# Opening of a hybrid attention and state-space layer: first weight unit laid out by k step, x and norm weights fetched on other queues, other splits and warm-up products

## The chip, the cores and the metric

The kernel runs on one core of one Trainium2 chip. The metric is the device time of one execution in microseconds (us). TensorE is called PE, VectorE DVE, ScalarE ACT, GpSimd POOL and SyncE SP, as in the profile. SP, ACT and POOL each have a queue on which they issue DMA transfers.

## The reference, cut to what matters

One layer on `x` of 256 rows by 2048 columns, batch 1, all in float32:

```python
hn = rms_norm(x, norm_w)
proj = hn @ w_in          # 2048 x 20544: q, k, v, z_a, z_s, xbc, dt, g_a, g_s
...                       # three dilated attentions, a convolution and a chunked state scan
merged = sigmoid(g_a) * (o_a @ w_attn_branch) + sigmoid(g_s) * (y @ w_ssm_branch)
return rms_norm(x + merged @ w_out, final_norm_w)
```

The change touches only the first product with `w_in`: 512 of its columns (one block of 128 for each of B, C, x and z of the state-space branch), against all 2048 rows of the contraction.

## The kernel before

**Weights and splits.** All weights lie in one array `wall` of units of 128 x 1024 floats (512 KB). Every unit is fetched by one transfer on SP's queue (`load`, L267) into one of five buffers `w`. As the products work in `fp32r`, a rounded form, each unit is split: ACT writes the rounded part `h` (L278) and DVE the remainder `l` (L279). The activations are split likewise into a high and a low half that lie side by side, 256 columns each. For each block of 128 x 128 weights PE then does one product of `h` with both halves (512 columns) and one of `l` with the high half alone (256 columns).

**The first gemm.** `gemm_first` does the 512 columns in eight units. A unit holds two k steps, a k step being 128 rows of the contraction: its first 512 columns are the first step's, the other 512 the second's. A k step is eight products, `h` at L385 and `l` at L386, for four accumulators. The first four units are split in halves, a k step each (`N_FINE`). For each k step the x block must have been fetched (`xr`), scaled with that step's column of the norm weights `pk` and split: ACT writes the high half (L286), DVE the low half (L290). These are the tiles `yTa` and `yTb`. The row norm itself is applied later.

**The order at the start.** Transfers are issued in the order of the code: on SP's queue the norm weights `pk`, then in turn a half of unit 0, an x block, the other half, and so on; the first x block alone goes on ACT's queue (`N_ACT_X`). Before the data arrives PE does `N_WARM` products with a tile of zeros, `ssq`, that DVE sets. A scheduler sets each engine's order within the limits of the data; `in_order` keeps an instruction's place in the program.

Of the kernel before, what the change touches and what calls it, by code (L numbers as in the profile page):

```python
# [9 lines left out]
F32 = mybir.dt.float32  # L10
F32R = mybir.dt.float32r
AF = mybir.ActivationFunctionType
ALU = mybir.AluOpType
PSUM = bass.MemoryType.PSUM

P = 128
S = 256
# [6 lines left out]
KT = D // P  # L24
UNIT = 1024
UK = 8
UB = 2
# [2 lines left out]
M_AHEAD = 200  # L30
T_LAGS = 1, 1
W_BUFS, H_BUFS = 5, 4
N_WARM = 4
X_CUTS = ((0, 1), (1, 2), (2, 4), (4, 6), (6, 8), (8, 10))
N_FINE = 4
N_ACT_X = 1
DT_LAG, CB_LAG, TURN_LAG, Y_LAG, S_LAG, M_LAG = 2, 8, 3, 11, 2, 2
# [88 lines left out]
FIRST = {}  # L126
# [6 lines left out]
def lay_weights(mats):  # L133
    out = np.empty((N_UNITS, P, UNIT), np.float32)
    for tag, form, src, off, n_kt, w in PLAN:
        if form == "m":
            m = np.concatenate([mats[src][:, o : o + P] for o in off], axis=1)
        else:
            m = mats[src][:, off : off + w]
        uk = UNIT // w  # L140
        n = n_kt // uk
        if form == "p":


            m = m.reshape(n // 2, 2, P, 2, 512)
            for q in range(n // 2):
                f = FIRST[tag] + 2 * q
                if q in S_QUADS[tag]:
                    out[f] = np.concatenate([m[q, 0, :, 0], m[q, 1, :, 0]], axis=1)
                    out[f + 1] = np.concatenate([m[q, 0, :, 1], m[q, 1, :, 1]], axis=1)  # L150
                else:
                    out[f : f + 2] = m[q].reshape(2, P, UNIT)
            continue
        out[FIRST[tag] : FIRST[tag] + n] = m.reshape(n, uk, P, w).transpose(0, 2, 1, 3).reshape(n, P, UNIT)
    return out


# [41 lines left out]
def hybrid_block(ctx: ExitStack, tc: tile.TileContext, wall, xt, x, pk_d, cst_d, fw_d, out):  # L199
    nc = tc.nc  # L200
    ve, ac, gp, pe = nc.vector, nc.scalar, nc.gpsimd, nc.tensor
    in_order = tc.keep_in_program_order
# [9 lines left out]
    pk = lead.tile([P, N_PK], F32, name="pk", tag="pk")  # L212
# [13 lines left out]
    def bank(tag, bufs, name):  # L226
        return ps.tile([P, 512], F32, name=name, tag=tag, bufs=bufs)

    loaded = {}
# [7 lines left out]
    def ring(name):  # L237
        return stream.tile([P, UNIT], F32, name=name, tag="w", bufs=W_BUFS)
# [24 lines left out]
    def load(n, cuts=(0, UNIT)):  # L263
        if n not in loaded:
            loaded[n] = stream.tile([P, UNIT], F32, name=f"w{n}", tag="w", bufs=W_BUFS)
        for a, b in zip(cuts, cuts[1:]):
            nc.sync.dma_start(loaded[n][:, a:b], wall[n, :, a:b])  # L267

    def unit(n, shape):
        if n not in loaded:  # L270
            load(n)
        w = loaded.pop(n)
        h = stream.tile([P, UNIT], F32R, name=f"h{n}", tag="h", bufs=H_BUFS)
        l = stream.tile([P, UNIT], F32R, name=f"l{n}", tag="l", bufs=H_BUFS)
        cuts = (0, UNIT // 2, UNIT) if n < N_FINE else (0, UNIT)
        with tc.high_priority(L_AHEAD) if n >= KT // UB else nullcontext():
            for a, b in zip(cuts, cuts[1:]):
                ac.activation(h[:, a:b], w[:, a:b], AF.Copy)  # L278
                ve.tensor_tensor(l[:, a:b], w[:, a:b], h[:, a:b].bitcast(F32), ALU.subtract)  # L279
        for f in on_unit.pop(n, ()):  # L280
            f(h[:, 0:1].bitcast(F32))
        k, m = shape
        return h.rearrange("p (k m) -> p k m", k=k), l.rearrange("p (k m) -> p k m", k=k)

    def split(src, hi, lo, scale=1.0):
        ac.activation(hi, src, AF.Copy, scale=scale)  # L286
        if isinstance(scale, float):
            ve.tensor_tensor(lo, src, hi.bitcast(F32), ALU.subtract)
        else:
            ve.scalar_tensor_tensor(lo, src, scale, hi.bitcast(F32), ALU.mult, ALU.subtract)  # L290
# [4 lines left out]
    def kt_of(t, kt):  # L295
        return t[kt // 8][:, kt % 8, :] if isinstance(t, list) else t[:, kt, :]
# [21 lines left out]
    def tick(final=False):  # L318
        now[0] += 1
        run_due(float("inf") if final else now[0])  # L320

    def gemm_a(tag, xs_of, acc=None):
        run = 2 if tag in IN_TWOS else 1
        held = in_order if tag not in FREE else lambda ins: None
        tick()
        name = f"{tag[0]}{tag[1]}"
        acc = bank(acc, 2, f"ps_{name}") if acc else bank("g", 4, f"ps_{name}")
        for u in range(KT // UK):
            h, l = unit(FIRST[tag] + u, (UK, P))
            for k0 in range(0, UK, run):  # L330
                for kk in range(k0, k0 + run):
                    kt = u * UK + kk
                    high = pe.matmul(acc, h[:, kk, :], xs_of(kt), start=(kt == 0), stop=False)  # L333
                    if kt == 0:
                        held(high)
                        run_due(now[0] + 0.5)
                for kk in range(k0, k0 + run):
                    kt = u * UK + kk
                    low = pe.matmul(acc[:, S:], l[:, kk, :], xs_of(kt)[:, :S], start=False, stop=(kt == KT - 1))  # L339
        held(low)  # L340
        return acc
# [25 lines left out]
    def project(tag, acc=None):  # L367
        return gemm_a(tag, lambda kt: XT[:, kt, :], acc)

    def gemm_first(tag, prepare, load_on):  # L370
        name = f"{tag[0]}{tag[1]}"
        accs = [bank("g", 4, f"ps_{name}_{j}") for j in range(4)]
        for u in range(KT // UB):
            if u % 2 == 0:
                tick()
            for kk in range(UB):
                prepare(u * UB + kk)
            h, l = unit(FIRST[tag] + u, (UB, 512))
            load_on(u)
            for kk in range(UB):  # L380
                kt = u * UB + kk
                m = kt_of(yT, kt)
                for j, acc in enumerate(accs):
                    js = slice(j * P, (j + 1) * P)
                    pe.matmul(acc, h[:, kk, js], m, start=(kt == 0), stop=False)  # L385
                    pe.matmul(acc[:, S:], l[:, kk, js], m[:, :S], start=False, stop=(kt == KT - 1))  # L386
        return accs

    def evac(acc, out_ap, name, scale=1.0):
# [228 lines left out]
    xr = big.tile([P, KT, S], F32, name="xr", tag="yo1a")  # L618
# [3 lines left out]
    def half_kts(name, tag):  # L622
        return big.tile([P, KT // 2, 2 * S], F32R, name=name, tag=tag)

    yT = [half_kts(f"yT{n}", f"yo0{n}") for n in "ab"]
    ssq = cpool.tile([P, 2, S], F32, name="ssq", tag="ssq")
    ve.memset(ssq, 0.0)
    warm = bank("m2", 2, "warm")
    for _ in range(N_WARM):
        pe.matmul(warm[:, :S], ssq[:, 0, :P], ssq[:, 0], start=True, stop=True)  # L630
    th_s = big.tile([P, 2, D], F32, name="th_s", tag="sgs")
    nc.sync.dma_start(pk[:, :KT], pk_d[:, :KT])
    for n, (a, b) in enumerate(X_CUTS):
        (nc.scalar if n < N_ACT_X else nc.sync).dma_start(xr[:, a:b, :], xt[:, a:b, :])
        if n < 2:
            load(0, (n * UNIT // 2, (n + 1) * UNIT // 2))
        elif n < 5:
            load(n - 1)
    ac.activation(a_neg, half[:SH, 0:1], AF.Exp)

    def split_x(kt):
        split(xr[:, kt], kt_of(yT, kt)[:, :S], kt_of(yT, kt)[:, S:], scale=pk[:, kt : kt + 1])

    def fetch(dst, src, behind, queue=nc.sync):
        gp.tensor_copy(dst[:, 0:1], behind)
        queue.dma_start(dst, src)
# [7 lines left out]
    def load_on(u):  # L654
        if u:
            load(u + 4)
        if u < 3:
            nc.sync.dma_start(xr[:, 2 * u + 10 : 2 * u + 12, :], xt[:, 2 * u + 10 : 2 * u + 12, :])
        if u == 3:
            nc.sync.dma_start(pk[:, KT:], pk_d[:, KT:])  # L660
# [31 lines left out]
    with tc.tile_pool(name="ssm", bufs=2) as sp:  # L692
# [175 lines left out]


        accs = gemm_first(("first", 0), split_x, load_on)  # L870
        raws = [collect(acc, f"first{j}") for j, acc in enumerate(accs[:3])]
        first = {n: new_pair(0, n) for n in ("xs", "zs")}
# [50 lines left out]
        for g in range(GROUPS):  # L923
# [9 lines left out]
            for t in range(max(4 * g, 1), 4 * g + 4):  # L933
                u, i = divmod(t, 2)
                acc = project(("xs", t))
# [19 lines left out]
                acc = project(("zs", t))  # L955
# [88 lines left out]
    with tc.tile_pool(name="att", bufs=2) as ap:  # L1044
# [55 lines left out]
        for h in range(NH):  # L1100
            q, k = (ap.tile([P, S], F32, name=f"{n}T{h}", tag=f"{n}T", bufs=2) for n in "qk")
# [3 lines left out]
            p = ap.tile([P, 384], F32, name=f"p{h}", tag="p", bufs=2)  # L1105
# [21 lines left out]
    with tc.tile_pool(name="fin", bufs=2) as fp:  # L1127
# [36 lines left out]
        for n in range(4):  # L1164
            i, cs = n // 2, slice(n % 2 * UNIT, (n % 2 + 1) * UNIT)
            behind_unit(
                FIRST[X_BEHIND[n][0]] + X_BEHIND[n][1],
                lambda behind, i=i, cs=cs: fetch(fin[:, i, cs], x[i * P : (i + 1) * P, cs], behind, nc.scalar),
# [3 lines left out]
        for n, (tag, u) in enumerate(FW_BEHIND):  # L1172
            cs = slice(n * UNIT, (n + 1) * UNIT)
# [12 lines left out]
        for c0 in (0, 2):  # L1186
# [17 lines left out]
            for i in range(2):  # L1204
                f = fs[:, i, :9]
                for c, acc in zip((c0, c0 + 1), es[2 * i : 2 * i + 2]):
                    cs = slice(c * 512, (c + 1) * 512)
# [28 lines left out]
        for i in range(2):  # L1236
            r = fs[:, i, 7:8]
            for c in (3, 0, 2, 1) if i else (3, 0, 1, 2):
                cs = slice(c * 512, (c + 1) * 512)
# [43 lines left out]
```

## Time and profile before

| | us |
|---|---|
| median of three runs | 1380.45 |
| lowest, highest | 1379.41, 1380.56 |
| the profiled execution's own time | 1379.87 |
| its span, first to last instruction | 1378.0 |

The profile is of one execution, the 1379.87 us one; 1.87 us of it lie outside its span. All times of rows count from the span's start. PE is busy for 1366.8 us of the span (99%), DVE for 1177.0, ACT for 840.0, POOL for 161.7. The granted clock of TensorE is told in the profile as a share of 2.4 GHz.

### The profile page before, as it was taken

How to read it: one execution, taken by the hardware profiler on the slowest of the kernel's cores; microseconds unless marked ns; L12 is line 12 of the kernel's file. 1: busy time of each engine (PE TensorE's matmuls, PEld its weight loads, DVE VectorE, ACT ScalarE, POOL GpSimd, SP SyncE). 2: the span in 40 equal slices, each digit the busy share in tenths (PEclk: the TensorE clock that was granted, in tenths of full speed). 3: DMA queues.
4: the chain of work that ended last, by engine and by line, in shares of the span. 5: the costliest groups of instructions: out<-in, count | busy, mean ns of one | idle time of the engine just before them, and what ended most of it. 6: DMA issues, size and time to landing. Idle time of an engine off the chain costs nothing.

```text
span 1378.0 us, 20734 instructions
## 1 busy us (share of the span) xinstructions
PE 1366.8 (99%) x7260; PEld 1164.8 (85%) x7260; DVE 1177.0 (85%) x1763; ACT 840.0 (61%) x1310; POOL 161.7 (12%) x238
## 2 busy tenths in 40 slices
PE   9999999999999999999999999999999999999997
PEld 7888888888888888888888888888888888888886
DVE  6898899898899888788989888777877789988897
ACT  7655777675667676666565554454444557655564
POOL 2301211101020100010001001211211000400112
PEclk9999999999999999999999999999999999999999
DMA  9767878778787867578677568888889757875773
GB/s 342 237 190 237 298 267 286 262 244 288 248 277 237 298 203 220 174 242 277 228 261 270 211 215 316 306 275 280 306 298 302 230 163 267 291 244 173 246 273 122
DMA packets 106520, 348.15 MB, mean 253 GB/s; under 512 B 11888, under 2 KB 14256, under 8 KB 106416
## 3 DMA queue, kind: packets, MB, share of 16 engines
q1 hardware_dynamic: 104400, 340.67, 74.0%
q10 hardware_dynamic: 1440, 4.06, 0.8%
q0 software_dynamic: 576, 2.10, 0.4%
q8 instruction: 57, 0.93, 0.3%
q14 instruction: 47, 0.39, 0.1%
HBM read 316.97 MB, written 29.82 MB: 252 GB/s over the span
## 4 chain that ended last, share of the span: by engine, by line
PE 98%; DMA 0%; DVE 0%; ACT 0%; issue 0%; SPq 0%; POOL 0%; POOLq 0%; DVEq 0%
PE ps_xs L333 8%; PE ps_zs L333 8%; PE ps_k L333 4%; PE ps_za L333 4%; PE ps_q L333 4%; PE ps_zs L339 4%; PE ps_xs L339 4%; PE ps_ssm L485 3%; PE ps_ssm L486 3%; PE ps_ssm L484 3%; PE ps_q L339 2%; PE ps_za L339 2%; PE ps_k L339 2%; PE ps_gs L421 2%; PE ps_gs L422 2%; PE ps_gs L420 2%
## 5 line engine op out<-in xcount | busy, mean ns | idle before, releaser
L278 ACT ACTIVATE h<-w 128x1024 fp32r<-128x1024 f32 (+1 forms) x394 | 410.0, 1048 | 306.0 <-issue 73.7
L279 DVE TENSOR_TENSOR l<-w,h 128x1024 fp32r<-128x1024 f32 (+1 forms) x394 | 474.0, 1209 | 111.1 <-ACT h L278 106.9
L333 PE MATMUL ps_zs<-XT,h 128*128 128x512 f32 x496 | 172.0, 393 | 0.0
L333 PE MATMUL ps_xs<-XT,h 128*128 128x512 f32 x496 | 171.6, 393 | 0.0
L339 PE MATMUL ps_zs<-XT,l 128*128 128x256 f32 x496 | 134.6, 279 | 0.0
L339 PE MATMUL ps_xs<-XT,l 128*128 128x256 f32 x496 | 133.7, 277 | 0.0
L333 PEld LDWEIGHTS ps_xs<-XT,h 128*128 128x128 f32 x496 | 91.3, 188 | 19.4
L333 PEld LDWEIGHTS ps_zs<-XT,h 128*128 128x128 f32 x496 | 91.3, 188 | 18.9
L339 PEld LDWEIGHTS ps_zs<-XT,l 128*128 128x128 f32 x496 | 93.3, 188 | 2.1
L339 PEld LDWEIGHTS ps_xs<-XT,l 128*128 128x128 f32 x496 | 93.2, 188 | 2.1
L333 PE MATMUL ps_q<-XT,h 128*128 128x512 f32 x256 | 91.1, 404 | 0.0
L333 PE MATMUL ps_k<-XT,h 128*128 128x512 f32 x256 | 88.6, 395 | 0.0
L333 PE MATMUL ps_za<-XT,h 128*128 128x512 f32 x256 | 88.4, 394 | 0.0
L551 ACT ACTIVATE ha<-wa 128x1024 fp32r<-128x1024 f32 x45 | 47.5, 1056 | 45.9 <-PE ps_ssm L486 10.0
L339 PE MATMUL ps_q<-XT,l 128*128 128x256 f32 x256 | 68.4, 278 | 0.0
L339 PE MATMUL ps_k<-XT,l 128*128 128x256 f32 x256 | 68.4, 277 | 0.0
L339 PE MATMUL ps_za<-XT,l 128*128 128x256 f32 x256 | 68.4, 277 | 0.0
L552 DVE TENSOR_TENSOR la<-wa,ha 128x1024 fp32r<-128x1024 f32 x45 | 54.8, 1218 | 8.4 <-ACT ha L551 8.3
L552 DVE TENSOR_TENSOR ltu<-wa,htu 128x1024 fp32r<-128x1024 f32 x40 | 48.7, 1219 | 10.8 <-ACT htu L551 10.8
L793 ACT ACTIVATE gt<-acb,acT 128x128 f32<-128x128 f32 x128 | 44.1, 390 | 22.2 <-DMA acb<-acum_d 21.9
L333 PEld LDWEIGHTS ps_k<-XT,h 128*128 128x128 f32 x256 | 47.0, 188 | 9.9
L333 PEld LDWEIGHTS ps_q<-XT,h 128*128 128x128 f32 x256 | 47.1, 188 | 9.7
(691 smaller groups left out, 3347.8 us busy)
## 6 DMA issues: line engine op xcount, KB each, us to landing
w<-in_wall SPq DMA_DIRECT2D x390, 512.0 KB, 4.8
wa<-in_wall SPq DMA_DIRECT2D x45, 512.0 KB, 4.7
th_a<-in_wall SPq DMA_DIRECT2D x21, 512.0 KB, 4.7
sums_at<-in_wall SPq DMA_DIRECT2D x18, 512.0 KB, 5.0
acb<-acum_d SPq DMA_DIRECT2D x32, 256.0 KB, 3.8
t_ssm<-sums_at SPq DMA_DIRECT2D x13, 512.0 KB, 4.3
wt<-t_ssm SPq DMA_DIRECT2D x13, 512.0 KB, 4.7
th_a<-in_wall SPq DMA_DIRECT2D x21, 256.0 KB, 5.4
```

The source lines that it names most:

```text
L278: ac.activation(h[:, a:b], w[:, a:b], AF.Copy)
L279: ve.tensor_tensor(l[:, a:b], w[:, a:b], h[:, a:b].bitcast(F32), ALU.subtract)
L333: high = pe.matmul(acc, h[:, kk, :], xs_of(kt), start=(kt == 0), stop=False)
L339: low = pe.matmul(acc[:, S:], l[:, kk, :], xs_of(kt)[:, :S], start=False, stop=(kt == KT - 1))
L420: pe.matmul(accs[i], xh, h[:, kk], start=(kt == 0), stop=False)
L421: pe.matmul(accs[i], xh, l[:, kk], start=False, stop=False)
L484: pe.matmul(acc, xh, h, start=start, stop=False)
L485: pe.matmul(acc, xh, l, start=False, stop=False)
L486: pe.matmul(acc, xl, h, start=False, stop=stop)
L551: ac.activation(h, src, AF.Copy)
L552: ve.tensor_tensor(l, src, h.bitcast(F32), ALU.subtract)
L793: ac.activation(g4[:, n, b], acb[:, j, b // 2 * P : b // 2 * P + P], AF.Relu, scale=-1.0, bias=sc[:, h : h + 1],)
```

## The change

- **Unit 0** lies in `wall` by k step: the 128 x 512 floats of its first k step are one run of 256 KB, then those of the second. Before, the two steps' rows of 2 KB alternated. Each half is still one transfer of 256 KB.
- **x** blocks 0 and 1 come in one transfer of 256 KB on ACT's queue, instead of one of 128 KB there and one on SP's.
- **Norm weights** `pk` (8 KB) are issued by POOL's queue instead of SP's.
- **Splits of x blocks 0 and 1** are both done by DVE: a multiplication with a scalar for the high half, in the place of ACT's, then the low half as before. DVE's order in unit 0 is written out: high, low, `l` for the first step, then for the second.
- **Products** of the first two k steps are written in a fixed order: four with `h`, then four with `l`.
- **Warm-up:** six products of 128 x 128 instead of four of 128 x 256, on a part of the zeros that is set first; the other zeros are set behind them.

```diff
-N_WARM = 4
-X_CUTS = ((0, 1), (1, 2), (2, 4), (4, 6), (6, 8), (8, 10))
+N_WARM = 6
+X_CUTS = ((0, 2), (2, 4), (4, 6), (6, 8), (8, 10))
...
+        if form == "m":
+            out[FIRST[tag]] = m[: uk * P].reshape(P, UNIT)
...
-            for a, b in zip(cuts, cuts[1:]):
+            for i, (a, b) in enumerate(zip(cuts, cuts[1:])):
+                if ahead:
+                    ahead(i)
                 ac.activation(h[:, a:b], w[:, a:b], AF.Copy)
-                ve.tensor_tensor(l[:, a:b], w[:, a:b], h[:, a:b].bitcast(F32), ALU.subtract)
+                low = ve.tensor_tensor(l[:, a:b], w[:, a:b], h[:, a:b].bitcast(F32), ALU.subtract)
+                if ahead:
+                    in_order(low)
...
-    ve.memset(ssq, 0.0)
+    ve.memset(ssq[:, 0, :P], 0.0)
     warm = bank("m2", 2, "warm")
     for _ in range(N_WARM):
-        pe.matmul(warm[:, :S], ssq[:, 0, :P], ssq[:, 0], start=True, stop=True)
+        pe.matmul(warm[:, :P], ssq[:, 0, :P], ssq[:, 0, :P], start=True, stop=True)
+    ve.memset(ssq[:, 0, P:], 0.0)
+    ve.memset(ssq[:, 1], 0.0)
     th_s = big.tile([P, 2, D], F32, name="th_s", tag="sgs")
-    nc.sync.dma_start(pk[:, :KT], pk_d[:, :KT])
+    gp.dma_start(pk[:, :KT], pk_d[:, :KT])
+    loaded[0] = ring("w0")
+    steps = wall[0].rearrange("(k p) (q m) -> k (p q) m", k=2, q=2)
+    for k in range(2):
+        nc.sync.dma_start(loaded[0][:, k * 512 : k * 512 + 512], steps[k])
     for n, (a, b) in enumerate(X_CUTS):
         (nc.scalar if n < N_ACT_X else nc.sync).dma_start(xr[:, a:b, :], xt[:, a:b, :])
-        if n < 2:
-            load(0, (n * UNIT // 2, (n + 1) * UNIT // 2))
-        elif n < 5:
-            load(n - 1)
+        if 0 < n < 4:
+            load(n)
     ac.activation(a_neg, half[:SH, 0:1], AF.Exp)
 
     def split_x(kt):
+        if kt < 2:
+            hi, lo = kt_of(yT, kt)[:, :S], kt_of(yT, kt)[:, S:]
+            in_order(ve.tensor_scalar(hi, xr[:, kt], pk[:, kt : kt + 1], None, ALU.mult))
+            ve.scalar_tensor_tensor(lo, xr[:, kt], pk[:, kt : kt + 1], hi.bitcast(F32), ALU.mult, ALU.subtract)
+            return
         split(xr[:, kt], kt_of(yT, kt)[:, :S], kt_of(yT, kt)[:, S:], scale=pk[:, kt : kt + 1])
```

SP's queue at the start, before: `w_93` is unit 0, `w_98` unit 1, `w_101` unit 2, `w_104` unit 3.

```order
L632 DMA pk<-in_pk 128x16
L267 DMA w_93<-in_wall 128x512
L634 DMA xr<-in_xt 128x256
L267 DMA w_93<-in_wall 128x512
L634 DMA xr<-in_xt 128x512
L267 DMA w_98<-in_wall 128x1024
L634 DMA xr<-in_xt 128x512
L267 DMA w_101<-in_wall 128x1024
```

The same place after the change: `w_96` is unit 0, `w_101` unit 1, `w_104` unit 2.

```order
L652 DMA w_96<-in_wall 128x512 x2
L654 DMA xr<-in_xt 128x512
L269 DMA w_101<-in_wall 128x1024
L654 DMA xr<-in_xt 128x512
L269 DMA w_104<-in_wall 128x1024
L654 DMA xr<-in_xt 128x512
```

Two transfers of the first five are gone from this queue, so unit 1 stands fourth in it instead of sixth; the others keep their order.

DVE at the start, before: zeros, then low halves of x and remainders `l` in turn.

```order
L627 MEMSET ssq 128x512
L290 SCALAR_TENSOR_TENSOR yTa<-xr,pk,yTa 128x256
L279 TENSOR_TENSOR l_131<-w_93,h_130 128x512
L290 SCALAR_TENSOR_TENSOR yTa<-xr,pk,yTa 128x256
L279 TENSOR_TENSOR l_131<-w_93,h_130 128x512
L290 SCALAR_TENSOR_TENSOR yTa<-xr,pk,yTa 128x256 x2
L279 TENSOR_TENSOR l_161<-w_98,h_160 128x512 x2
```

DVE at the start, after: `l_130` is of unit 0, `l_164` of unit 1.

```order
L641 MEMSET ssq 128x128
L645 MEMSET ssq 128x128
L646 MEMSET ssq 128x256
L662 TENSOR_SCALAR yTa<-xr,pk 128x256
L663 SCALAR_TENSOR_TENSOR yTa<-xr,pk,yTa 128x256
L283 TENSOR_TENSOR l_130<-w_96,h_129 128x512
L662 TENSOR_SCALAR yTa<-xr,pk 128x256
L663 SCALAR_TENSOR_TENSOR yTa<-xr,pk,yTa 128x256
L283 TENSOR_TENSOR l_130<-w_96,h_129 128x512
L296 SCALAR_TENSOR_TENSOR yTa<-xr,pk,yTa 128x256 x2
```

The multiplications of x blocks 0 and 1 have come from ACT to DVE, where each now stands ahead of its low half. On every engine the order of the rest of the program is the same as before but for a few neighbours that change places: the last transfers of x and two of the norm's products among them.

## Rows read from the trace of the kernel before

**Rows 1.** The page: the chain of work that ended last, by engine.

```profile
PE 98%; DMA 0%; DVE 0%; ACT 0%; issue 0%; SPq 0%; POOL 0%; POOLq 0%; DVEq 0%
```

**Rows 2.** PE alone in two stretches: length, busy (instructions), granted clock, DMA share, GB/s.

```profile
0.00:9.53 9.53, 6.73 (x25) 1.00 0.77 231
9.53:34.00 24.47, 24.47 (x133) 1.00 1.02 385
```

**Rows 3.** The chain that ended last, first 40 us: start, us, what.

```profile
3.07 5.75 DMA w<-in_wall
8.85 0.64 ACT h L278
9.53 1.20 PE ps_first L385 x4
...
12.60 0.93 PE ps_first L385 x4
13.53 0.47 PE ps_first L386 x4
```

**Rows 4.** Timeline: start, us, engine, line, operation, [idle time before it and its releaser].

```profile
0.72 0.10 POOL L224 MEMSET half<- 128x2 f32 x1 [0.29 <-POOLq L1273]
...
0.73 0.39 SPq L632 DMA_DIRECT2D pk<-in_pk  x1
...
1.18 0.41 SPq L267 DMA_DIRECT2D w<-in_wall  x1
...
1.44 3.68 PE L630 MATMUL warm<-ssq 128*128 128x256 f32 x8 [1.44 <-DVE ssq L627]
...
3.79 0.48 DVE L290 SCALAR_TENSOR_TENSOR yTa<-xr,pk,yTa 128x256 fp32r<-128x256 f32 x1 [2.40 <-ACT yTa L286]
3.87 0.63 ACT L278 ACTIVATE h<-w 128x512 fp32r<-128x512 f32 x1
...
4.54 0.69 DVE L279 TENSOR_TENSOR l<-w,h 128x512 fp32r<-128x512 f32 x1 [0.27 <-ACT h L278]
...
4.66 1.39 PE L385 MATMUL ps_first<-yTa,h 128*128 128x512 f32 x4
...
6.81 1.19 PE L385 MATMUL ps_first<-yTa,h 128*128 128x512 f32 x4 [0.29 <-ACT h L278]
```

**Rows 5.** DMA issues near 0.73, 1.18, 3.07 and 4.02 us: KB, us to landing.

```profile
pk<-in_pk SPq DMA_DIRECT2D x1, 8.0 KB, 2.3
...
w<-in_wall SPq DMA_DIRECT2D x1, 256.0 KB, 2.7
...
w<-in_wall SPq DMA_DIRECT2D x1, 512.0 KB, 5.8
...
w<-in_wall SPq DMA_DIRECT2D x1, 512.0 KB, 7.2
```

**Rows 6.** Four stretches, all engines: busy (instructions), then granted clock, DMA share, GB/s.

```profile
1.80:2.25 0.45, 0.45 (x2) 0.36 (x2) 0.00 (x0) 0.45 (x1) 0.00 (x0) 1.00 0.51 103
2.50:3.50 1.00, 1.00 (x4) 0.82 (x3) 0.00 (x0) 0.43 (x2) 0.00 (x0) 1.00 0.99 358
3.50:5.00 1.50, 1.50 (x6) 1.20 (x5) 0.95 (x2) 1.01 (x3) 0.43 (x1) 1.00 0.94 202
5.00:9.00 4.00, 3.17 (x17) 2.41 (x15) 2.29 (x5) 2.08 (x5) 0.27 (x1) 1.00 0.96 298
```

**Rows 7.** DMA issues of the whole span by line: 512 KB from POOL's queue and from SP's.

```profile
sx_x<-sxd_x SPq DMA_DIRECT2D x5, 512.0 KB, 5.1
...
sx_o<-sxd_o POOLq DMA_DIRECT2D x4, 512.0 KB, 7.9
```

**Rows 8.** Groups by line and shape on DVE: count, busy us, mean ns of one.

```profile
L1070 DVE TENSOR_SCALAR p<-p,st 128x256 f32<-128x256 f32 x16 | 5.6, 347 | 0.0
```

**Rows 9.** Groups of weight loads in the first 40 us.

```profile
L385 PEld LDWEIGHTS ps_first<-yTb,h 128*128 128x128 f32 x32 | 5.7, 188 | 1.0
...
L630 PEld LDWEIGHTS warm<-ssq 128*128 128x128 f32 x8 | 2.5, 331 | 2.0 <-DVE ssq L627 1.4
```

More of the change, by code (lines that the diff above doesn't have):

```diff
@@ L267, in load, with unit @@
             nc.sync.dma_start(loaded[n][:, a:b], wall[n, :, a:b])
-    def unit(n, shape):
+    def unit(n, shape, ahead=None):
         if n not in loaded:
@@ L375, in gemm_first @@
                 tick()
-            for kk in range(UB):
-                prepare(u * UB + kk)
-            h, l = unit(FIRST[tag] + u, (UB, 512))
+            if u:
+                for kk in range(UB):
+                    prepare(u * UB + kk)
+            h, l = unit(FIRST[tag] + u, (UB, 512), prepare if u == 0 else None)
             load_on(u)
@@ L382, in gemm_first @@
                 m = kt_of(yT, kt)
[L383 to L386, printed above, removed]
+                per = 4 if kt < 2 else 1
+                for j0 in range(0, 4, per):
+                    js = [(accs[j], slice(j * P, (j + 1) * P)) for j in range(j0, j0 + per)]
+                    for acc, cs in js:
+                        high = pe.matmul(acc, h[:, kk, cs], m, start=(kt == 0), stop=False)
+                        if kt < 2:
+                            in_order(high)
+                    for acc, cs in js:
+                        low = pe.matmul(acc[:, S:], l[:, kk, cs], m[:, :S], start=False, stop=(kt == KT - 1))
+                        if kt < 2:
+                            in_order(low)
         return accs
@@ L626, in hybrid_block @@
     ssq = cpool.tile([P, 2, S], F32, name="ssq", tag="ssq")
-    ve.memset(ssq, 0.0)
+    ve.memset(ssq[:, 0, :P], 0.0)
     warm = bank("m2", 2, "warm")
     for _ in range(N_WARM):
-        pe.matmul(warm[:, :S], ssq[:, 0, :P], ssq[:, 0], start=True, stop=True)
+        pe.matmul(warm[:, :P], ssq[:, 0, :P], ssq[:, 0, :P], start=True, stop=True)
+    ve.memset(ssq[:, 0, P:], 0.0)
+    ve.memset(ssq[:, 1], 0.0)
     th_s = big.tile([P, 2, D], F32, name="th_s", tag="sgs")
-    nc.sync.dma_start(pk[:, :KT], pk_d[:, :KT])
+    gp.dma_start(pk[:, :KT], pk_d[:, :KT])
[3 more added lines that the diff above has]
+        nc.sync.dma_start(loaded[0][:, k * 512 : k * 512 + 512], steps[k])
     for n, (a, b) in enumerate(X_CUTS):
         (nc.scalar if n < N_ACT_X else nc.sync).dma_start(xr[:, a:b, :], xt[:, a:b, :])
-        if n < 2:
-            load(0, (n * UNIT // 2, (n + 1) * UNIT // 2))
-        elif n < 5:
-            load(n - 1)
+        if 0 < n < 4:
+            load(n)
     ac.activation(a_neg, half[:SH, 0:1], AF.Exp)
     def split_x(kt):
+        if kt < 2:
+            hi, lo = kt_of(yT, kt)[:, :S], kt_of(yT, kt)[:, S:]
+            in_order(ve.tensor_scalar(hi, xr[:, kt], pk[:, kt : kt + 1], None, ALU.mult))
+            ve.scalar_tensor_tensor(lo, xr[:, kt], pk[:, kt : kt + 1], hi.bitcast(F32), ALU.mult, ALU.subtract)
+            return
         split(xr[:, kt], kt_of(yT, kt)[:, :S], kt_of(yT, kt)[:, S:], scale=pk[:, kt : kt + 1])
```

## Prediction

> **What bounds the kernel now.** I read the chain of work that ended last first, since an edit counts only where it shortens that chain. 98% of it is PE [rows 1]: the kernel is a queue of products, and whatever lets PE begin its unbroken run earlier moves everything behind it. So the second view is PE by stretch. From 9.53 to 34 us PE is busy for all 24.47 us; from the start to 9.53 us it is busy for 6.73, and warm-up products on zeros are in that [rows 2]. The opening ends at 9.53 us, where the third k step begins, and only what moves that moment can move the end.
>
> Third, the chain in order of time says what sets 9.53: unit 1, issued at 3.07, is on its way for 5.75 us; ACT rounds its first half for 0.64; PE starts [rows 3]. The first two k steps are not on it. Step 0 starts at 4.66 and step 1 at 6.81 [rows 4]. With the 1.40 us (0.93 + 0.47) that a step takes later in the same gemm [rows 3], they are 2.8 us of work that has from 4.66 to 9.53 to be done. PE's start could slip until 9.53 - 2.80 = 6.7 us and cost nothing, if step 1 could follow at once.
>
> Fourth, why unit 1 takes that long. A 256 KB half of unit 0, second on an empty queue, lands after 2.7 us [rows 5], so 5.8 us is no property of the transfer. The DMA engines are 94 to 99% busy from 2.5 us to 9 [rows 6]: the bytes ahead are the wait. Ahead of unit 1's last byte stand `pk` (8 KB), x blocks 0 to 3 (512 KB), unit 0 (512 KB) and unit 1 itself (512 KB), 1544 KB. The rate is uneven: 103 GB/s from 1.80 to 2.25, 358 to 3.5, 202 to 5.0, 298 to 9 [rows 6].
>
> **The change, part by part.**
>
> *Fewer issues on SP.* `pk` and x block 1 leave the queue. Their issues stood 0.45 us apart from the next (0.73 to 1.18 [rows 4]); unit 1 is issued at about 3.07 - 0.90 = 2.15. That is worth nothing by itself, for the engines behind the queue are busy then. What counts is the first entry: the first half of unit 0 is issued at 0.73 instead of 1.18, and x blocks 0 and 1, 256 KB, at 0.73 on ACT's queue. So the weak stretch from 1.80 to 2.25 fills up. At 358 instead of 103 GB/s it moves (358 - 103) x 0.45 = 115 KB more, which at the 298 GB/s of later is 0.39 us. The bytes ahead of unit 1 are 1536 KB instead of 1544: nothing. **Term 1: -0.4 us**, bounds 0 (what fills the stretch is as slow as what it replaces) and -0.45 (the whole shift of the issue).
>
> *Layout of unit 0.* Same bytes and transfers, but each is one run in memory. No row shows what a run is worth. The stretch from 3.5 to 5.0, in which the second half moves, has 202 GB/s against 358 just before: (358 - 202) x 1.5 = 234 KB, 0.79 us at 298 GB/s. Bounds 0 (the drop has another cause) and -0.79 (all of it is the alternating rows). The first half alternated as well and moved within the 358 stretch, so I stay near zero: **term 2: -0.1 us**.
>
> *x blocks 0 and 1 split by DVE.* ACT loses two operations of some 0.5 us, which it did while waiting for weights. DVE's chain for step 0 becomes high (0.35, by the same shape in the attention [rows 8]), low (0.48), and for step 1 `l` of step 0 (0.69 [rows 4]), high, low: step 0 can start 0.35 + 0.48 + some 0.1 = 0.9 us after the later of `pk` and the x transfer, step 1 after 0.35 + 0.48 + 0.69 + 0.35 + 0.48 + 0.1 = 2.45. Step 1 is behind that and not behind step 0's end (0.9 + 1.40 = 2.3), so both are done 3.85 us after that moment. Call it P. ACT rounds unit 0 beside it.
>
> *When is P?* x: two transfers of 256 KB fill the engines from 1.8 us on; 524 kB at 358 GB/s is 1.5 us and the signal some half us, so 3.8 to 3.9. `pk`: POOL issues it after `half` is set, at 0.82 [rows 4]. The lower bound is SP's 2.3 us [rows 5]: 3.1. For the upper, 512 KB from POOL's queue land after 7.9 us and from SP's after 5.1 [rows 7]; all of that 2.8 as POOL's surplus gives 0.82 + 2.3 + 2.8 = 5.9. I take the middle, P = 4.5. Then step 0 starts at 5.4, later than the 4.66 of now, and both steps are done at 8.35. Unit 1's first half is ready at 9.53 - 0.5 = 9.0, so this is covered by 0.7 us: **term 3: 0**, bounds 0 (P up to 5.2) and +0.2 against now (P = 5.9: done at 9.75, over 9.53). The Trainium skill, SBUF — State Buffer, in the box on the trap "DVE blocks DMA", says that a POOL-issued transfer can wait for its descriptors while DVE runs certain copies. At the time of this issue DVE has only zeros to set, so by it the sum would stay the same; no row of this trace shows the case.
>
> *Warm-up.* The smaller products start when a quarter of the zeros is set. Each now takes 3.68 / 8 = 0.46 for 256 columns [rows 4]; twelve of half the columns are 2.8 us, from about 1.1 to 3.9. They do not stand before step 0 at 5.4. What they leave is a gap of 1.5 us on PE, which I come back to as a rival. **Term 4: 0.** The order of the products within a step is what PE runs anyway for the first steps (four, then four [rows 4]): 0.
>
> *Behind the opening.* The next step that could stall is step 4, due at 9.53 + 2.80 = 12.33. Unit 2 lands at 4.02 + 7.2 = 11.2 [rows 5] and needs 0.63 on ACT: 11.9, a slack of 0.4. It moves earlier with the same bytes, so the gain is kept. The rest of the program is in the same order but for neighbours, and I carry the gain to the end one for one; the bounds are the same.
>
> **Sum:** -0.4 - 0.1 = -0.5 us. Against the profiled execution, 1379.87 becomes 1379.4. That execution lies 0.58 under the median, so for the median 1380.45 - 0.5 = **1379.9**.
>
> **Rivals.**
>
> *A, nothing moves.* The merged transfers share the same engines, and unit 1 lands at 8.85 as now. For it: the share of 94 to 99% [rows 6]. Against it: the stretch at 103 GB/s with a share of 0.51. Time 1380.4. The Trainium skill, DMA: Bandwidth & Descriptors, under "Issuing engines are not separate DMA queues", states this rule: issuing on several engines saves only the sequencer's time. The share from 2.5 us on agrees.
>
> *B, the opening fills.* The drop to 202 GB/s was the alternating rows, and the rate holds at 358 from 1.8 us: 1573 kB (1536 KB) in 4.4 us, unit 1 lands about 6.7. Then the first two steps are the limit: 8.35 with P = 4.5, 7.75 with P = 3.9. Gain 1.2 to 1.8: 1378.7 to 1379.3. Against it: 5 to 9 us, where full units already move, shows 298 only.
>
> *C, slower: PE's clock.* The granted clock reads 1.00, its 2.4 GHz level, in every stretch of the opening, but the warm-up's weight loads take 331 ns against 188 later [rows 9], as at the 1.2 GHz level; the level rises while PE works. If after 2.8 us of warm-up and the gap steps 0 and 1 run at half rate, they take 2.8 each: from 5.4 to 11.0, against 9.53 now: +1.5, 1381.9. It decides from the point where the full level comes after 8.1 us: half rate until then and 1.40 per step behind it ends at 9.53. For it: less zeros-work than the 3.7 us of now, and a gap. Against it: the warm-up starts earlier, and the four products of step 0, at 1.39 us [rows 4], are under the 1.86 of half rate (2 x 0.93) although they follow the zeros directly.
>
> *D, slower: `pk` late.* P over 5.7 makes the first two steps end after 9.53; at 5.9 it is +0.2: 1380.6.
>
> **Chances.** The sum within a few tenths: 0.45. A: 0.20. B: 0.20. C: 0.08. D: 0.07. About 0.2% (2.8 us) is what a measurement of this kernel can tell from no change, and no case alone reaches it: even PE working without a gap from 4.66 would gain 9.53 - 7.46 = 2.1. So faster 0.04 (B with drift of the runs), slower 0.03 (C with drift), same 0.93. The range takes in B's 1378.7 and most of C, and the runs' own scatter of 0.6: 1378.5 to 1381.2.
>
> **What would show it.** Right: the third step's first product at 9.0 to 9.2 with ACT's rounding of unit 1 as its releaser, unit 1 landing 0.3 to 0.5 us earlier, PE unbroken behind it; term 3: step 0 near 5.4, released by DVE's low half. Wrong: the releaser of step 2 is DVE or PE's own step 1 (D, or B), or weight loads of 331 ns in steps 0 and 1 (C), or stalls at step 4 that return the gain.

## The result and the profile after

| us | before | after |
|---|---|---|
| median of 11 runs each | 1380.56 | 1383.37 |
| lowest, highest | 1379.41, 1381.57 | 1381.91, 1385.07 |
| the profiled execution: time | 1379.87 | 1381.97 |
| its span | 1378.0 | 1380.1 |

The ratio after to before is 1.0021, 95% interval 1.0013 to 1.0029: 2.8 us slower by the medians, where 0.5 us faster was forecast, and outside the range (1378.5 to 1381.2). The no-change bound of 0.2% lies within the interval. The profiled execution is one of the quickest of the 11; its loss is 2.1 us.

First the page's chain of work that ended last, by engine, against [rows 1].

```profile
PE 97%; DVE 1%; DMA 1%; issue 1%; ACT 0%; POOL 0%; POOLq 0%; DVEq 0%; ACTq 0%
```

DVE, DMA and issue read 1% each now, where they read 0%. That is no measure of the opening. The chain leaves PE once more, from 1156 us on, through some 10 us of DVE's work and one transfer (start, us, what):

```profile
1169.94 5.01 DMA wa<-in_wall
1175.06 1.07 ACT ha L565
1176.17 0.50 PE pp_ga L498
```

PE itself is idle for 0.25 us there, just before 1176.17. PE in the two stretches of [rows 2]: length, busy (instructions), granted clock, DMA share, GB/s.

```profile
0.00:9.53 9.53, 5.55 (x20) 1.00 0.77 275
9.53:34.00 24.47, 24.47 (x136) 1.00 0.96 359
```

From 9.53 to 34 us PE is unbroken, as before; yet it has begun later, and its first stretch has 5.55 us of work against 6.73. What it waited for is in the chain in order of time (start, us, what), against [rows 3].

```profile
1.27 4.59 DMA pk<-in_pk
5.86 0.03 issue
5.89 0.36 DVE yTa L662
6.25 0.03 issue
6.28 0.49 DVE yTa L663
6.77 0.14 issue
6.91 2.04 PE ps_first L394 x4
8.95 0.85 PE ps_first L398 x4
9.80 1.21 PE ps_first L394 x4
```

The chain no longer goes through unit 1 and ACT. It goes from POOL's issue of the norm weights through DVE's two operations to step 0 at 6.91 us, and from there on PE itself is the chain. The timeline of the same stretch has what the chain leaves out.

```profile
1.04 2.93 PE L644 MATMUL warm<-ssq 128*128 128x128 f32 x12 [1.04 <-DVE ssq L641]
...
1.27 0.79 POOL L648 DMA_DIRECT2D pk<-in_pk  x1 [0.45 <-issue]
...
6.87 1.35 PEld L394 LDWEIGHTS ps_first<-yTa,h 128*128 128x128 f32 x4 [3.20 <-ACT h L282]
6.91 2.04 PE L394 MATMUL ps_first<-yTa,h 128*128 128x512 f32 x4 [2.93 <-DVE yTa L663]
...
8.01 1.15 ACT L282 ACTIVATE h<-w 128x512 fp32r<-128x512 f32 x2 [0.63 <-DMA w<-in_wall]
...
8.32 1.18 PEld L398 LDWEIGHTS ps_first<-yTa,l 128*128 128x128 f32 x4
...
9.60 1.41 PE L394 MATMUL ps_first<-yTa,h 128*128 128x512 f32 x4
...
10.62 0.66 PEld L398 LDWEIGHTS ps_first<-yTa,l 128*128 128x128 f32 x4
...
11.32 1.08 PE L394 MATMUL ps_first<-yTa,h 128*128 128x512 f32 x4
```

Three things stand here. The warm-up ends at 3.97, and PE is idle for 2.93 us. Four weight loads of step 0 then take 1.35 us, 338 ns each, about as long as the warm-up's 330 and not the 188 ns of later [rows 9]; four of L398 take 1.18, and 0.66 only at 10.62. So step 0 lasts 9.60 - 6.91 = 2.69 us and step 1 1.72, against 1.40 at the full level. And unit 1 is there early: ACT starts on it at 8.01, against 8.85 before, and step 2, which waited for it then, starts at 11.32 against 9.53. That is +1.79 us; the span grew by 2.1, and the 0.25 us at 1176 are most of the rest. The landing times (KB each, median us from the issue), first of the issues from 0.7 to 1.4 us, then of unit 1's at 2.11:

```profile
w<-in_wall SPq DMA_DIRECT2D x2, 256.0 KB, 4.3
xr<-in_xt ACTq DMA_DIRECT2D x1, 256.0 KB, 4.4
pk<-in_pk POOLq DMA_DIRECT2D x1, 8.0 KB, 4.6
...
w<-in_wall SPq DMA_DIRECT2D x1, 512.0 KB, 5.9
```

`pk` lands at 1.27 + 4.59 = 5.86, x at 0.73 + 4.4 = 5.13. The 8 KB took 2.3 us from SP's queue [rows 5].

### The profile page after: what moved, and what is told of

The parts are those of the page before. It is cut to its first block, busy times and chain, and to the rows that moved or that the text cites. A ratio compares the mean times of both kernels' runs of the same rounds, so it can differ in the third digit from the quotient of the medians.

```text
span 1380.1 us, 20741 instructions
## 1 busy us (share of the span) xinstructions
PE 1367.3 (99%) x7264; PEld 1166.8 (85%) x7264; DVE 1178.0 (85%) x1767; ACT 838.6 (61%) x1308; POOL 157.1 (11%) x239
## 3 DMA queue, kind: packets, MB, share of 16 engines
q10 hardware_dynamic: 1440, 4.19, 0.8%
q0 software_dynamic: 608, 2.11, 0.4%
## 4 chain that ended last, share of the span: by engine, by line
PE 97%; DVE 1%; DMA 1%; issue 1%; ACT 0%; POOL 0%; POOLq 0%; DVEq 0%; ACTq 0%
PE ps_xs L339 8%; PE ps_zs L339 8%; PE ps_za L339 4%; PE ps_k L339 4%; PE ps_q L339 4%; PE ps_zs L345 4%; PE ps_xs L345 4%; PE ps_ssm L499 3%; PE ps_ssm L500 3%; PE ps_ssm L498 3%; PE ps_q L345 2%; PE ps_k L345 2%; PE ps_za L345 2%; PE ps_gs L435 2%; PE ps_gs L436 2%; PE ps_gs L434 2%
```

## The experiments

Two faults can make the loss, and the runs separate them. *Late data*: `pk` comes late from POOL's queue, so step 0 starts late. *Slow PE*: the warm-up is too little or ends too early, so that steps 0 and 1 run at the 1.2 GHz level (W in the expectations). Each alone might cost nothing, since unit 1 is ready only near 9.5 us. The layout of unit 0 (L) and the merging of x are tested apart; the splits by DVE and the fixed order of products have no run of their own. The kernels tried have labels (e1, e2 and so on). The kernel before ran beside them: its median is 1380.74 us (33 runs) beside e2 to e5, 1380.94 (27) beside e1, e12 and e13, 1380.48 (33) beside e8 to e11. Each other kernel has 11 runs. The ratios, with their 95% intervals, are over all runs and can differ a little from the ratio of the medians.

**e2: more warm-up on the changed kernel.**

```diff
-N_WARM = 6
+N_WARM = 14
```

> The changed kernel with 14 warm-up products of 128 x 128 instead of 6, nothing else. Theory Q (two things add up: the norm weights land late on POOL's queue, at 5.86 us, and PE, idle from 3.97 to 6.91, does its first two k steps at half rate): the warm-up now lasts to 6 or 7 us, the norm weights are as late as before, step 0 starts at 6.9 to 7.1 but at full rate, so step 2 starts at about 9.8 instead of 11.32, 1.5 us are won back of the changed kernel's loss, some 0.2 to 1 us above the kernel before. Rival M (only the late data costs, the rate of the first two steps doesn't matter because unit 1 and DVE are the limit anyway): step 2 stays near 11.3, time as the changed kernel, +2.8. Rival X (longer warm-up stands in front of step 0): step 0 starts later than 7.2 and the time is above the changed kernel's.

1380.66 against 1380.74, ratio 1.0005 (0.9997 to 1.0014). Its timeline:

```profile
1.04 5.82 PE L644 MATMUL warm<-ssq 128*128 128x128 f32 x28 [1.04 <-DVE ssq L641]
...
5.90 0.35 DVE L662 TENSOR_SCALAR yTa<-xr,pk 128x256 fp32r<-128x256 f32 x1 [4.50 <-DMA pk<-in_pk]
...
6.89 0.76 PEld L394 LDWEIGHTS ps_first<-yTa,h 128*128 128x128 f32 x4 [0.22 <-issue]
6.92 1.16 PE L394 MATMUL ps_first<-yTa,h 128*128 128x512 f32 x4
...
8.38 1.08 PE L394 MATMUL ps_first<-yTa,h 128*128 128x512 f32 x4
...
9.77 1.09 PE L394 MATMUL ps_first<-yTa,h 128*128 128x512 f32 x4
```

`pk` is as late as in the changed kernel and step 0 starts at the same 6.92. But zeros fill PE up to there, the loads take 0.76 / 4 = 190 ns, and step 2 starts at 9.77 instead of 11.32. `N_WARM` alone gives back 1.55 us of the 1.79. The late data alone, with DVE's splits and the fixed order of products, which are in this kernel too, cost 9.77 - 9.53 = 0.24 us.

**e5: the norm weights first on ACT's queue, changed kernel otherwise.**

```diff
-    gp.dma_start(pk[:, :KT], pk_d[:, :KT])
+    nc.scalar.dma_start(pk[:, :KT], pk_d[:, :KT])
```

> The changed kernel with the norm weights on ACT's queue, ahead of the x transfer, instead of POOL's; nothing else. Theory Q: the norm weights land at about 3 us; step 0 then waits for the x transfer and unit 0's first half, which landed at 5.1 and 4.9 us in the changed kernel, and starts at 6.1 instead of 6.9; if PE is at full rate then, step 2 starts at 9.0 and the time is 0.5 us under the kernel before; if the gap behind the warm-up still leaves it at half rate, step 2 starts at 10.2 to 10.9 and the time is 0.7 to 1.4 us above. Rival W (the smaller warm-up alone makes the loss, the queue doesn't matter): the loss stays at 2 us or more.

1382.21, ratio 1.0012 (1.0003 to 1.0021): still slower. `pk` landed at 3.7, but x, now behind it on the queue, was issued at 1.17 and landed 4.2 us later, at 5.37. The timeline:

```profile
5.47 0.35 DVE L662 TENSOR_SCALAR yTa<-xr,pk 128x256 fp32r<-128x256 f32 x1 [4.07 <-DMA xr<-in_xt]
...
6.49 2.04 PE L394 MATMUL ps_first<-yTa,h 128*128 128x512 f32 x4 [2.52 <-DVE yTa L663]
...
11.75 1.17 PE L394 MATMUL ps_first<-yTa,h 128*128 128x512 f32 x4
```

Now x is what comes late. The gap of 2.5 us with the slow level behind it stayed, through both steps, so step 2 came later than the 10.2 to 10.9 expected for half rate.

**e1: the norm weights first on SP's queue, changed kernel otherwise.** The same line, with `nc.sync.dma_start`.

> The changed kernel with the norm weights first on SP's queue, nothing else: six warm-up products as in the change. Theory Q with what the runs before this one showed (late data alone +0.1 us, a small warm-up alone -0.3 to +0.3, both +2.8): the merged x transfer lands at 3.7 us, unit 0's first half at 4.4, step 0 is ready at about 5.1, a gap of 1.1 us behind the warm-up, half rate in steps 0 and 1 and so 2.8 us each: step 2 at 9.9 to 10.7, between +0.4 and +1.2 us, clearly under the changed kernel. Rival K (POOL's queue alone is the loss): all of it comes back, 0 to -0.5 us. Rival C (the small warm-up alone is the loss): it stays at +2 or more.

1380.83 against 1380.94, ratio 1.0002 (0.9993 to 1.0010). DVE can start on x at 4.17. Step 0 waits for unit 0's first half, which lands at 4.82 and is then rounded, and starts at 5.53:

```profile
5.53 1.35 PEld L394 LDWEIGHTS ps_first<-yTa,h 128*128 128x128 f32 x4 [1.85 <-ACT h L282]
5.53 2.08 PE L394 MATMUL ps_first<-yTa,h 128*128 128x512 f32 x4 [1.55 <-ACT h L282]
...
9.73 1.08 PE L394 MATMUL ps_first<-yTa,h 128*128 128x512 f32 x4
```

This is the opposite half of e2. The slow level is there (338 ns), with the same warm-up, but 1.4 us less lateness leaves room for it: step 2 starts 0.2 us after that of before. By the time it was rival K whose forecast came true (all of the loss comes back); Q's 9.9 to 10.7 for step 2 was too late, as the full level came within step 1, at 8.57. K is not the whole, for e2 has `pk` on POOL's queue and loses next to nothing.

**e4: only the small warm-up, on the kernel before.**

```diff
-N_WARM = 4
+N_WARM = 6
...
-    ve.memset(ssq, 0.0)
+    ve.memset(ssq[:, 0, :P], 0.0)
...
-        pe.matmul(warm[:, :S], ssq[:, 0, :P], ssq[:, 0], start=True, stop=True)
+        pe.matmul(warm[:, :P], ssq[:, 0, :P], ssq[:, 0, :P], start=True, stop=True)
+    ve.memset(ssq[:, 0, P:], 0.0)
+    ve.memset(ssq[:, 1], 0.0)
```

> The kernel before with one part of the change: six warm-up products of 128 x 128 on the part of the zeros that is set first. Rival W (the smaller warm-up by itself leaves PE at half rate): weight loads of 331 ns and more in steps 0 and 1, step 0 from 4.6 to 7.4, step 1 to 10, step 2 at about 10.1 instead of 9.53, +0.6 us or more. Theory Q: the gap of 0.6 us between warm-up and step 0 is too short to matter, steps 0 and 1 at full rate from about 5 us on, step 2 at 9.53, time within 0.2 us of the kernel before.

1381.08, ratio 1.0001 (0.9992 to 1.0010). Its timeline:

```profile
4.50 1.35 PEld L385 LDWEIGHTS ps_first<-yTa,h 128*128 128x128 f32 x4 [0.83 <-ACT h L278]
4.50 2.07 PE L385 MATMUL ps_first<-yTa,h 128*128 128x512 f32 x4 [0.53 <-ACT h L278]
...
7.23 1.86 PE L385 MATMUL ps_first<-yTa,h 128*128 128x512 f32 x4
...
9.40 1.08 PE L385 MATMUL ps_first<-yTa,h 128*128 128x512 f32 x4
```

After 2.93 us of zeros and a gap of half a us PE is at the slow level (338 ns a load), step 0 lasts 2.73 us, and nothing is lost: step 2 starts at 9.40. W was right about the level and Q about the time. PE has no idle time left ahead of step 2, so the reserve is used up.

**e3: only the norm weights on POOL's queue, on the kernel before.** The line of e1 the other way round (`nc.sync` to `gp`).

> The kernel before with one part of the change: the norm weights on POOL's queue. Theory Q: they land at 4.5 to 5.9 us instead of 3.0, the first x split on ACT and with it step 0 slip from 4.66 to 5.5 to 7; the larger warm-up lasts to 5.1, so steps 0 and 1 run at full rate, and step 2 starts at 9.3 to 9.9: between -0.2 and +0.4 us. If the gap behind the warm-up is enough for half rate, up to +1.8. Rival W: no change from the queue, step 0 at 4.7, time within 0.2 us.

1381.60, ratio 1.0005 (0.9996 to 1.0014): the time can't tell it from no change, the profile can. `pk` took 3.3 us and landed at 4.6. The timeline:

```profile
1.44 3.78 PE L630 MATMUL warm<-ssq 128*128 128x256 f32 x8 [1.44 <-DVE ssq L627]
...
5.85 0.80 PE L385 MATMUL ps_first<-yTa,h 128*128 128x512 f32 x1 [0.62 <-DVE yTa L290]
...
8.58 1.91 PE L385 MATMUL ps_first<-yTa,h 128*128 128x512 f32 x4
...
10.99 1.08 PE L385 MATMUL ps_first<-yTa,h 128*128 128x512 f32 x4
```

The late `pk` makes the gap itself, even behind the longer warm-up: 0.62 us of idle, then step 0 at half rate (2.73 us), and step 2 at 10.99, 1.46 late. So in this kernel the late data bring the slow level with them.

**e8: both faults mended.** e1 with `N_WARM = 14`.

> The changed kernel with the norm weights first on SP's queue and 14 warm-up products of 128 x 128. Theory Q says that the full rate and the late data are two separate conditions: the norm weights land at 3 us, the merged x transfer at about 5.1, step 0 starts at 6.0 to 6.2 at full rate, step 2 at about 9.0 (two steps of 1.40 behind it), 0.5 us under the kernel before. Rival M2 (the merged x transfer costs nothing): step 0 starts at 5 or earlier, step 2 at unit 1's landing, 8.5, 1 us under. Rival N (the order of arrival doesn't matter, DMA sets step 2): 9.5, no change against the kernel before.

1380.12 against 1380.48, ratio 0.9996 (0.9987 to 1.0004). x landed at 3.7, steps 0 and 1 ran at 5.77 and 7.25 at full rate, and PE then waited 1.55 us for unit 1, which landed at 9.66: step 2 at 10.36, later than any of the three expectations. That profiled execution is the slowest of its 11 (1382.23), so its place of step 2 is no typical one.

**e9: x blocks apart again, both on ACT's queue; the norm weights between the halves of unit 0 on SP's; warm-up of ten.**

```diff
-N_WARM = 6
-X_CUTS = ((0, 2), (2, 4), (4, 6), (6, 8), (8, 10))
+N_WARM = 10
+X_CUTS = ((0, 1), (1, 2), (2, 4), (4, 6), (6, 8), (8, 10))
-N_ACT_X = 1
+N_ACT_X = 2
...
-    gp.dma_start(pk[:, :KT], pk_d[:, :KT])
...
+        if k == 0:
+            nc.sync.dma_start(pk[:, :KT], pk_d[:, :KT])
```

> The changed kernel with x blocks 0 and 1 as two transfers, both on ACT's queue, the norm weights on SP's queue between the halves of unit 0, and 10 warm-up products of 128 x 128. Theory Q: x block 0 and the norm weights land at 3.2 to 3.7 us, unit 0's first half at 3.5 to 4, step 0 starts at 4.7 to 5.2 without a gap behind the warm-up, at full rate; unit 1 lands at 7.7 to 8.2 and step 2 starts at 8.4 to 8.9: 0.6 to 1.1 us under the kernel before. Rival N: unit 1 lands at 8.9 as before and the time is within 0.3 us.

1380.04, ratio 0.9997 (0.9989 to 1.0006). Step 0 at 5.49, step 2 at 9.62 behind unit 1, which landed at 8.91: rival N, and not the 8.4 to 8.9 of Q for step 2.

**e10: only the layout of unit 0, on the kernel before.**

```diff
+            out[FIRST[tag]] = m[: uk * P].reshape(P, UNIT)
...
-            nc.sync.dma_start(loaded[n][:, a:b], wall[n, :, a:b])
+            src = wall[n, :, a:b]
+            if n == 0:
+                k = a // (UNIT // 2)
+                src = wall[0].rearrange("(k p) (q m) -> k (p q) m", k=2, q=2)[k]
+            nc.sync.dma_start(loaded[n][:, a:b], src)
```

> The kernel before with one part of the change: unit 0 laid out by k step, everything else as it was. If the layout is what took the rate of the DMA engines from 202 to 391 GB/s in the stretch from 3.5 to 5 us (theory L), unit 1 lands at 8.0 to 8.3 instead of 8.87 and step 2 starts at 8.7 to 9.0, some 0.5 to 0.8 us under the kernel before. If the rate has another cause (rival S: the earlier start of unit 0 and x), unit 1 lands at 8.7 to 8.9, time within 0.3 us.

1380.92, ratio 1.0003 (0.9994 to 1.0012). The stretch that the layout was to help, all engines: busy (instructions), granted clock, DMA share, GB/s.

```profile
3.50:5.00 1.50, 1.50 (x6) 1.11 (x4) 0.85 (x2) 1.06 (x3) 0.34 (x1) 1.00 0.80 222
```

222 GB/s against 202 [rows 6], and unit 1 landed at 3.06 + 6.15 = 9.21, not earlier than before. The changed kernel has 391 there, so the layout by itself isn't what fills this stretch.

**e11: only x blocks 0 and 1 in one transfer, on the kernel before.** The halves of unit 0 then stand next to each other.

```diff
-X_CUTS = ((0, 1), (1, 2), (2, 4), (4, 6), (6, 8), (8, 10))
+X_CUTS = ((0, 2), (2, 4), (4, 6), (6, 8), (8, 10))
...
-        if n < 2:
-            load(0, (n * UNIT // 2, (n + 1) * UNIT // 2))
-        elif n < 5:
-            load(n - 1)
+        if n == 0:
+            load(0, (0, UNIT // 2, UNIT))
+        elif n < 4:
+            load(n)
```

> The kernel before with one part of the change: x blocks 0 and 1 in one transfer of 256 KB on ACT's queue, and the halves of unit 0 next to each other on SP's. Theory Q: the merged transfer lands at about 4.5 to 5 us instead of 3.2 for block 0, ACT's two splits come first in its order and unit 0's rounding behind them, step 0 starts at 6 to 6.6; with the large warm-up that ends at 5.1 the rate of the first steps depends on the execution: +0.2 us if full, up to +1.8 if half. Rival M2 (merging costs nothing): step 0 at 4.7 to 5.0, time within 0.3 us.

1380.05 against 1380.48, ratio 0.9998 (0.9989 to 1.0007). Its timeline:

```profile
5.35 0.76 PEld L385 LDWEIGHTS ps_first<-yTa,h 128*128 128x128 f32 x4 [0.84 <-ACT h L278]
...
8.13 1.15 ACT L278 ACTIVATE h<-w 128x512 fp32r<-128x512 f32 x2 [0.72 <-DMA w<-in_wall]
...
8.81 1.21 PE L385 MATMUL ps_first<-yTa,h 128*128 128x512 f32 x4 [0.39 <-ACT h L278]
```

Unit 1 is rounded from 8.13, 0.72 earlier than before, and step 2 starts 0.72 earlier; the time shows 0.4 us by the medians, which the interval doesn't tell from none. The merging need not be the cause. It also takes a transfer off SP's queue, so that unit 1 is issued at 2.59 instead of 3.07, and e3, which takes only `pk` off that queue and leaves x apart, has an earlier unit 1 as well, and the same stretch filled (its timeline, then the stretch):

```profile
8.44 1.15 ACT L278 ACTIVATE h<-w 128x512 fp32r<-128x512 f32 x2 [1.03 <-DMA w<-in_wall]
...
3.50:5.00 1.50, 1.50 (x5) 0.82 (x3) 0.29 (x1) 0.95 (x2) 0.26 (x1) 1.00 1.11 344
```

Over all profiles the start of ACT on unit 1 goes with unit 1's issue:

| unit 1 issued at, us | ACT starts on it at | GB/s from 3.5 to 5.0 | profiles |
|---|---|---|---|
| 3.06 to 3.07 | 8.61 to 9.30 | 173 to 222 | before, e4, e10, e13 |
| 2.58 to 2.60 | 8.13 to 8.94, once 9.68 (e8) | 283 to 344 | e1, e3, e8, e9, e11, e12 |
| 2.11 | 7.74 to 8.36 | 322 to 396 | after (both), e2, e5 |

**e13 and e12: ten small warm-up products, on the kernel before and on e11** (the edit of e4 with `N_WARM = 10`, and both edits together).

> The kernel before with ten warm-up products of 128 x 128 on zeros that are set first: PE works from 1.04 to about 5 us instead of 1.44 to 5.1. If the kernel before loses time in some executions to half rate (the reason of its scatter of 3 us), the median falls by 0.3 us and the runs over 1381 get rare. If its scatter has another cause, no change: within 0.2 us, same scatter.

> A candidate for a version that beats both: the kernel before with x blocks 0 and 1 merged (1380.05 against 1380.48 us by itself) and ten warm-up products of 128 x 128 that start at 1.04 us. Step 0 is ready at 5.35 us, the warm-up ends at about 5.0 to 5.3, full rate; step 2 at unit 1's landing plus 0.65, 8.8 us: 0.4 to 0.8 us under the kernel before. If the order of arrival in that one profile was luck, no change.

e13: 1380.89 against 1380.94, ratio 1.0005 (0.9995 to 1.0014), step 0 at 5.33, step 2 at 9.98. Four of its 11 runs are over 1382.8 us. Its profile, of another run, has steps 0 and 1 almost wholly at the full level, so it doesn't say what made those four long. e12: 1380.54, ratio 0.9998 (0.9989 to 1.0007), step 2 at 8.96. No version beats the kernel before by more than can be measured.

**The changed kernel once more,** beside e1.

> The changed kernel once more, for a second profile: its median lies 0.7 us further from the kernel before than its first profiled execution did. Theory Q: the norm weights land at 5.9 us again, step 0 at 6.9, and how long steps 0 and 1 run at half rate varies: step 2 anywhere from 10.5 (full rate early in step 0) to 12.5 us (half rate through both). Rival: all is as in the first profile, step 2 at 11.3, and what varies lies behind the opening.

1382.50, span 1380.6. Its timeline:

```profile
1.27 0.79 POOL L648 DMA_DIRECT2D pk<-in_pk  x1 [0.45 <-issue]
...
5.49 0.35 DVE L662 TENSOR_SCALAR yTa<-xr,pk 128x256 fp32r<-128x256 f32 x1 [4.08 <-DMA pk<-in_pk]
...
8.99 1.40 PEld L394 LDWEIGHTS ps_first<-yTa,h 128*128 128x128 f32 x4
9.20 1.91 PE L394 MATMUL ps_first<-yTa,h 128*128 128x512 f32 x4
...
11.76 1.27 PE L394 MATMUL ps_first<-yTa,h 128*128 128x512 f32 x4
```

`pk` came 0.4 us sooner and step 0 at 6.50, but step 1 too ran at half rate (its loads take 350 ns). Step 2 starts at 11.76: +2.23 us. The page reads PE 98% and DVE and DMA 0% here, as before the change, although the opening is the longer one.

## Why the prediction was wrong

The runs, one profile each, make a table of step 2's start:

| step 2 starts at, us | PE at the full level in steps 0 and 1, but for the start | at half rate in step 0 at least |
|---|---|---|
| step 0 at about 4.6 | 9.53 (before) | 9.40 (e4) |
| step 0 at about 6.9 | 9.77 (e2) | 11.32 (after) |

Late data alone cost 0.24 us, the slow level alone nothing, both together 1.79. The times say the same: by the medians e2 is 0.1 us under the kernel before and e4 0.3 above, neither told from none, and the changed kernel 2.8 above. The two share one reserve: unit 1 is ready only near 9.5, and the 2.8 us of steps 0 and 1 have 4.66 to 9.53 to be done in [rows 4], which leaves 2.1 us. Either fault fits into these, not both. Nor do they come apart by themselves: where data are late and the warm-up isn't made longer, PE has a gap, and the slow level lasts beyond it (e3). In the eight profiles in which zeros last to within 0.2 us of step 0, the first weight load under 250 ns, that is at the full level, comes at 4.4 to 6.4 us; in the six with a gap of 0.5 to 2.9 us on PE it comes at 8.6 to 12.2. A gap that comes once the level is up did no such harm: e8's PE waits 1.55 us ahead of step 2 and goes on with four loads in 0.76 us.

**The step that failed** is term 3, "I take the middle, P = 4.5", and with it term 4, "They do not stand before step 0 at 5.4. What they leave is a gap of 1.5 us on PE", both put at 0. P was 5.86, in the second profile 1.27 + 4.19 = 5.46, at or near the upper bound. The working counted POOL's issue from 0.82; the engine idled another 0.45 us first and issued for 0.79, and the 8 KB landed 4.2 to 4.6 us after the start of the issue. x too came later than its 3.8 to 3.9: at 5.13, and at 5.37 in e5, where it set P. From P to step 0 went 1.05 us (0.9 forecast). Then the gap was not 1.5 but 2.93 us, and behind it the slow level came, rival C.

**The rivals were priced one at a time.** D gave late `pk` +0.2 us at P = 5.9; e2, which has just that, measured +0.24. C gave the slow level from 5.4 on +1.5, with a chance of 0.08. But a later P is also a longer gap, and starts the slow steps later: 5.9 + 0.9 + 2 x 2.8 = 12.4, +2.9 us. The profiles have 11.32 and 11.76, as the full level comes in step 1 or behind it. The two were one case, and the forecast had no chance for it. What the prediction held against C, that step 0's four products took 1.39 us and not 1.86, was no evidence: in before they follow without a gap. With 0.53 us of gap (e4) or 1.55 (e1), both behind 2.93 us of zeros, they took 2.07 and 2.08 us.

The Trainium skill, TensorE: Matmul & The Clock Gate, Part 1, says that the array starts at the lower clock, rises with sustained work, and that the number of slow products differs from run to run for the same kernel. The two profiles of the changed kernel agree: the first load under 250 ns comes at 10.38 us, within step 1, in one and at 12.18, behind it, in the other.

**Terms 1 and 2** together had the right sign: ACT starts on unit 1 at 8.01 instead of 8.85, -0.84 us against -0.5. But the cause of term 1 was not the one given. The stretch from 1.80 to 2.25, which was to fill up, moved 82 GB/s against 103; the gain came in 3.5 to 5.0, at 391 against 202 [rows 6]. By e10 that isn't the layout (term 2 has no effect that these runs show), and it isn't the merged x either, for e3 gets 344 GB/s without both. What the kernels with a full stretch share is unit 1's earlier issue, of which the prediction said "That is worth nothing by itself": issued 0.96 us earlier in the changed kernel, ACT starts on it 0.84 earlier. No run moves the issue and nothing else; that this is the cause is likely, not shown. The gain was worth nothing here, for PE was not ready for unit 1.

**What held.** The end follows PE's start: 1.79 us at step 2, 2.1 at the end of the span. PE is unbroken from step 0 to 900 us, and no stall at step 4 appeared. The chances for the sign (0.93 for no change) were too sure: C and D each stayed under the bound of 2.8 us, and the two added, +2.9, do not.

**What stays open.** The median's 2.8 us is more than the 1.8 and 2.2 us at step 2 in the two profiles; both lie under the median of 1383.37, and when the full level came in the other runs isn't seen. Every kernel here scatters by 2 to 4 us, and what sets that, e13's four long runs too, was not found. Part of it lies behind the opening: from step 2 to the end of the span before takes 1368.5 us, e8 and e10 1370.0. Why `pk` takes 4.2 to 4.6 us from POOL's queue in the changed kernel and 3.3 in e3 isn't settled: that its bytes wait behind two transfers of 256 KB, issued first at 0.73, is only argued.

## What to carry to other kernels

A reserve that hides two edits must be charged with both at once: add up the worst of each against the one slack before either is called free. Work that is to bring PE's clock up has to reach up to the first product that counts, so when data come later, the warm-up must grow by as much. And a small transfer that everything waits for belongs first in a queue whose latency the trace shows, not in one chosen because it is free.

## What the runs showed of the hardware

- The granted clock of the profile's rows reads 1.00, the 2.4 GHz level, from the start of the span, while weight loads of 338 ns show half rate until 10 us: in the opening the loads' durations tell the level, that column doesn't. The trace's own entries on the clock begin only where the full level comes, at 4.89 us in before, 6.15 in e2, 10.28 and 12.14 in the two profiles of the changed kernel, and the column counts the time ahead of them as 1.00. In all fourteen profiles the first load under 250 ns stands within 0.2 us of that entry.
- The same 8 KB from POOL's queue landed after 3.3, 4.2 and 4.6 us, from SP's after 2.2 to 3.2, from ACT's after 3.0. The Trainium skill, DMA: Bandwidth & Descriptors, "Anatomy of one DMA — SWDGE (gpsimd) path", has a fixed 2.0 us and bytes at 436 GB/s, by which 8 KB would take an estimated 2.02 us; the measured times, which hold 0.79 us of POOL's issuing, are 1.6 to 2.3 times that, and they decide.
- Two transfers of 256 KB issued at 0.73 on two queues both landed after 4.2 to 4.4 us (after; 3.7 to 3.9 in its second profile). Where `pk` went ahead of the one on SP's queue, x landed after 3.0 to 3.4 (e1, e8, e11, e12). That the two held each other up is argued, not shown.
